# Issuing the first load ahead of the opening barrier in a row-wise maximum-norm kernel

## The chip, the cores and the metric

The kernel runs on one core of one Trainium2 chip. TensorE, VectorE, ScalarE, GpSimd and SyncE are the five engines that have a row of instructions in its trace. The profile counts 16 DMA engines, which carry out the loads and stores in packets (3072 of 64 KB for the bulk loads); here SyncE issues all loads and the last store, ScalarE the two other stores. A barrier is a place in the program where every engine waits until all have reported; a drain is the instruction with which an engine comes to it (SyncE's starts at 0.00 us in the kernel before, and SyncE is released at 0.65). The metric is the device time of an execution in microseconds (us). The profile gives a second number, the span: from the first to the last instruction on record in one profiled execution. Device time and span differ by the same amount in the two profiled runs: 629.88 against 628.10 us before the change, 629.10 against 627.32 after it, which is 1.78 us both times.

## The reference

```python
def setup_inputs():
    return {"x": np.random.randn(8192, 8192).astype(np.float32)}   # rows, cols

def reference(x):
    return np.linalg.norm(x, ord=np.inf, axis=1)
```

`np.linalg.norm` with `ord=np.inf` and one axis is the largest absolute value of each row. The input is 268 MB and the output 32 KB, so the kernel is a stream of loads with one reduction behind it.

## The kernel before

A tile `t` holds two rows for each of 128 partitions (16384 float32 values a partition, 8.39 MB in all). SyncE issues the load, VectorE reduces it; there are three buffers. The first 48 rows of each partition (24 tiles) are the bulk; the last 16 rows are the tail, loaded and reduced in ever smaller pieces so that little work is left when the last data arrive.

```python
TAIL = (
    [[8192]] * 8
    + [[4096, 4096]] * 5
    + [[2048] * 4] * 2
    + [[2048, 2048, 2048, 1024, 512, 512]]
)
# ... (views of x and out; pools: sbuf has bufs=3)
    nc.vector.memset(part[:], 0.0)

    def absmax(o, i):
        nc.vector.reduce_max(out=o, in_=i, axis=X, apply_absolute_value=True)

    for a in range(A):
        for n in range(G):
            t = sbuf.tile([P, B * cols + 16], F32, tag="t")
            nc.sync.dma_start(out=t[:, : B * cols], in_=x_b[a, n])
            absmax(
                r_bulk[:, a, n * B : (n + 1) * B],
                t[:, : B * cols].rearrange("p (b c) -> p b c", b=B),
            )
    nc.scalar.dma_start(out=out_b, in_=r_bulk[:])
    # ... (the tail, in the pieces of TAIL, results into part and then r_tail, r_fin)
```

No line of the kernel function writes the opening barrier. The trace shows it ahead of the program, under the line that makes the program object (L114): GpSimd sets four constants (0.23 to 0.43 us), each engine runs a drain, the four others report with theirs (SyncE's starts at 0.00, TensorE's as the last of them at 0.32), and GpSimd collects the reports at 0.53 and releases the four at 0.61; SyncE goes on at 0.65.

## Time and profile before

| | before |
|---|---|
| device time, median of the first 3 runs | 629.97 us (629.90 to 630.30) |
| span of the profiled run | 628.10 us |
| SyncE released from the opening barrier | 0.65 us |
| first load issued / first packet | 0.73 / 1.75 us |
| bulk reduction starts, one to the next | 19.33 us on average |
| last data in | 623.22 us |
| from last data to the end of the span | 4.88 us |

The barrier's release, the packets and the last data are read from the single records of the trace; everything else is on the page and in the views below. First, lines of the profile page of the kernel before: the span, VectorE's busy time, the busy share of the DMA engines in 40 equal slices (9 is 90% or more), and the bytes moved.

```profile
span 628.1 us, 196 instructions
...
DVE 552.7 (88%) x58; POOL 0.2 (0%) x4
...
DMA  9999999999999999999999999999999999999996
...
HBM read 268.44 MB, written 0.03 MB: 427 GB/s over the span
```

The DMA engines are busy for 90% of the time or more in all slices but the last, where the program ends. From the packet records, the rate between 20 and 460 us is 433.9 GB/s. VectorE is the second busiest, at 88%.

The timeline of the kernel before, first 24 us. Columns are start, duration, engine with line and operation, then what ended the idle time before it. SPq is SyncE's queue of issues; one line may sum up several issues.

```profile
start us, us, engine line op out<-in xcount [idle before <-releaser]
...
0.73 1.33 SPq L68 DMA_DIRECT2D t<-in_x_dram  x3
0.81 0.11 DVE L60 MEMSET part<- 128x60 f32 x1 [0.81 <-PEq L114]
22.83 17.22 DVE L63 TENSOR_REDUCE r_bulk<-t 128x2 f32<-128x16384 f32 x1 [21.91 <-DMA t<-in_x_dram]
```

The first load is issued at 0.73 us, and VectorE then has nothing to do for 21.91 us. The wait view of the kernel before (waiter, line, what it waited for: total us, times, longest):

```profile
DVE r_bulk L63 <- DMA t<-in_x_dram: 70.5, 24, 21.9
```

Of the 70.5 us, the first wait is 21.9; the other 23 are some 2.1 us each. VectorE is ahead of the stream in every bulk tile. The chain of waits of the kernel before, its first pieces (start, duration, what):

```profile
0.66 0.07 issue
0.73 0.38 SPq L68
1.11 0.06 issue
1.17 40.92 DMA t<-in_x_dram
...
42.11 17.22 DVE r_bulk L63
```

Read this view with care. It enters the stream through the *second* load, issued at 1.17 and landed at 42.09, because that is the load for which VectorE waits at 42 us. For the first 20.8 of these 40.92 us the load stands in the queue behind the first one: by the packet records its own first packets start at 21.95 on average. The timeline's end, kernel before:

```profile
621.01 4.01 DVE L63 TENSOR_REDUCE t<-t 128x1 f32<-128x2048 f32 x3 [0.20 <-DMA t<-in_x_dram]
625.05 0.69 DVE L63 TENSOR_REDUCE r_fin<-t 128x1 f32<-128x517 f32 x1
625.77 0.35 SPq L99 DMA_DIRECT2D out_dram<-r_fin  x1
```

### The profile page before, as it was taken

The page shows a single profiled execution, that of the slowest core. Times are in us where ns is not written, and L with a number is a line of the kernel's source. Part 1 is how long each engine was busy: PE and PEld are TensorE (multiplying, and loading weights), DVE is VectorE, ACT ScalarE, POOL GpSimd, SP SyncE. Part 2 cuts the span into 40 slices and gives each one's busy share as a digit, 9 for nine tenths or more (in the row PEclk, how much of TensorE's full clock was granted, in tenths as well). Part 3 has the DMA queues.
Part 4 walks back from the last instruction along what each step waited for, and adds up shares of the span by engine and source line. Part 5 has one row for each costly group of instructions (what it writes and reads, how often), then busy time and mean ns, then how long its engine had stood idle before and what let it go on. Part 6 is the DMA issues. An engine that isn't in the chain of part 4 may idle for free.

```text
span 628.1 us, 196 instructions
## 1 busy us (share of the span) xinstructions
DVE 552.7 (88%) x58; POOL 0.2 (0%) x4
## 2 busy tenths in 40 slices
DVE  0588988889988889888898888998889999999998
POOL 0000000000000000000000000000000000000000
DMA  9999999999999999999999999999999999999996
GB/s 401 413 455 413 455 413 455 413 455 413 455 413 455 409 459 413 455 413 455 413 455 413 455 413 455 413 455 413 455 405 430 434 435 432 420 432 432 424 426 274
DMA packets 9138, 268.49 MB, mean 427 GB/s; under 512 B 1968, under 2 KB 1968, under 8 KB 2352
## 3 DMA queue, kind: packets, MB, share of 16 engines
q1 hardware_dynamic: 8208, 268.44, 99.1%
q10 hardware_dynamic: 928, 0.03, 0.1%
q14 instruction: 2, 0.02, 0.0%
HBM read 268.44 MB, written 0.03 MB: 427 GB/s over the span
## 4 chain that ended last, share of the span: by engine, by line
DMA 64%; DVE 30%; another core or an unknown queue 4%; issue 1%; SPq 0%
DMA t<-in_x_dram 64%; DVE r_bulk L63 23%; DVE part L63 5%; DVE t L63 1%; SPq L82 0%; DVE r_fin L63 0%; SPq L68 0%
## 5 line engine op out<-in xcount | busy, mean ns | idle before, releaser
L63 DVE TENSOR_REDUCE r_bulk<-t 128x2 f32<-128x16384 f32 x24 | 413.3, 17219 | 70.5 <-DMA t<-in_x_dram 70.5
L63 DVE TENSOR_REDUCE part<-t 128x1 f32<-128x4096 f32 (+2 forms) x26 | 130.0, 5067 | 1.3 <-DMA t<-in_x_dram 1.3
L63 DVE TENSOR_REDUCE t<-t 128x1 f32<-128x2048 f32 (+2 forms) x5 | 8.6, 1746 | 0.4 <-DMA t<-in_x_dram 0.4
L60 DVE MEMSET part<- 128x60 f32 x1 | 0.1, 108 | 0.8 <-PEq L114 0.8
L63 DVE TENSOR_REDUCE r_fin<-t 128x1 f32<-128x517 f32 x1 | 0.7, 692 | 0.0
L63 DVE TENSOR_REDUCE r_tail<-part 128x15 f32<-128x60 f32 x1 | 0.2, 216 | 0.0
L114 POOL MEMSET const-bfloat16-1.0<- 128x1 bf16 x1 | 0.1, 101 | 0.0
L114 POOL MEMSET const-uint8-127<- 128x1 uint8 x1 | 0.1, 101 | 0.0
L114 POOL MEMSET const-float32-0.0<- 128x1 f32 x1 | 0.1, 98 | 0.2 <-issue 0.2
L114 POOL MEMSET const-float32-1.0<- 128x1 f32 x1 | 0.1, 98 | 0.0
## 6 DMA issues: line engine op xcount, KB each, us to landing
t<-in_x_dram SPq DMA_DIRECT2D x8, 4096.0 KB, 37.0
t<-in_x_dram SPq DMA_DIRECT2D x10, 2048.0 KB, 30.4
t<-in_x_dram SPq DMA_DIRECT2D x11, 1024.0 KB, 24.6
t<-in_x_dram SPq DMA_DIRECT2D x1, 512.0 KB, 15.9
t<-in_x_dram SPq DMA_DIRECT2D x2, 256.0 KB, 13.2
t<-in_x_dram SPq DMA_DIRECT2D x24, 40.7
out_dram<-r_bulk ACTq DMA_DIRECT2D x1, 24.0 KB, 57.9
out_dram<-r_tail ACTq DMA_DIRECT2D x1, 7.5 KB, 5.6
```

Of the source, the lines that this page charges most:

```text
L60: nc.vector.memset(part[:], 0.0)
L63: nc.vector.reduce_max(out=o, in_=i, axis=X, apply_absolute_value=True)
L114: nc = _bacc.Bacc("TRN2", target_bir_lowering=False, num_devices=1)
```

## The change

The intent: no work of the first load depends on the barrier, so let SyncE issue it as its first instruction. After the program is built, a hook takes the first DMA instruction of SyncE out of its block, asserts that it waits for nothing, and puts it ahead of SyncE's first instruction.

```diff
+def start_first_load_early(nc):
+    sp = mybir.EngineType.SP
+    first, *rest = nc.main_func.blocks
+    for block in rest:
+        insts = block.instructions
+        for i, ins in enumerate(insts):
+            if ins.engine == sp and type(ins).__name__ == "InstDMACopy":
+                assert not ins.sync_info.on_wait
+                moved = insts[i]
+                block.instructions = insts[:i] + insts[i + 1 :]
+                head = first.instructions
+                at = next(k for k, h in enumerate(head) if h.engine == sp)
+                first.instructions = head[:at] + [moved] + head[at:]
+                return
 ...
     nc.sync.dma_start(out=out_t[:, n_tail - 1 :], in_=r_fin[:])
+    nc.at_finalize(start_first_load_early)
```

## The prediction

> **What bounds the kernel now.** The stream of loads. The page shows 268.44 MB in a 628.1 us span (427 GB/s), DMA at 9 tenths or more in all slices but the last. From the packet records, between 20 and 460 us the rate is 433.9 GB/s, one 8.39 MB tile per 19.3 us. [...] VectorE is busy 88%: a bulk reduction takes 17.22 us and then waits 2.1 us for its load (chain and wait views). Three loads are in flight, so when a buffer is released about one and a tenth tiles are still queued: from the first packet at 1.75 us to the last data at 623.2 us there is no moment at which all 16 DMA engines are idle.
>
> So the time is a sum: start to first packet (1.75 us), the stream (621.5 us), the fixed end after it (4.9 us: last reductions, output store, closing barrier), plus 1.8 us by which the device time of the profiled run (629.88) exceeds its span.
>
> **What the change does.** Only the first term changes. Before, SyncE starts at 0.00 with its drain, is released from the opening barrier at 0.65 and issues the first load at 0.73 (0.38 us in the sequencer, first packet 0.64 us after that). Now the load is SyncE's first instruction, at 0.00. The load waits for nothing. Added: SyncE reaches the barrier about 0.38 us later (its drain follows the load), near 0.45 us; GpSimd collects at 0.53 us only after its own memsets, so the barrier moves by 0 to 0.15 us. That delays only the second load, which has 20 us of slack behind the first, and VectorE's memset of the partial maxima, which is needed at 490 us. The second and third loads issue at about 0.75 and 1.2 us instead of 1.17 and 1.64.
>
> **Share on the critical path.** All of the 0.73 us: the stream never runs dry. That is 0.12% of 630 us. [...]
>
> **Predicted time:** 629.97 - 0.73 = 629.25 us; 8 in 10 between 628.95 and 629.8. Faster by over 2%: 0.3%; within 2%: 99.2%; slower by over 2%: 0.5%.
>
> **What the profile would show.** (1) First load at 0.00 in the timeline, first packet near 1.0 instead of 1.75, first reduction at 22.1 instead of 22.83, its first wait shorter by 0.7. (2) The same 19.3 us period, the last data 0.7 us earlier, the same 4.9 us end. (3) Span about 627.4 us. (4) SyncE released from the barrier at 0.65 to 0.8, the second load right after it.
>
> **What would make it wrong.** (a) SyncE's drain might wait for the load's completion, not just its issue: then barrier, second load and all else would be held some 20 us, the stream would have a hole of about 2 us, and the kernel would lose one to two us. (b) The first load may cost more to issue or to start when it is the very first instruction, eating some of the 0.73. (c) The profile's zero is SyncE's first instruction; the device time may begin elsewhere. (d) The gain is only about twice the spread of the three runs (0.4 us).

## The result and the profile after

| | before | after | difference |
|---|---|---|---|
| median device time, 6 runs each | 630.14 us (629.90 to 630.55) | 629.13 us (628.99 to 629.77) | |
| ratio | | 0.9986, 95% interval 0.9973 to 0.9999 | |
| span of the profiled run | 628.10 | 627.32 | -0.78 |
| first load issued | 0.73 | 0.00 | -0.73 |
| SyncE released from the barrier | 0.65 | 0.71 | +0.06 |
| second load issued | 1.17 | 0.79 | -0.38 |
| first packet | 1.75 | 1.02 | -0.74 |
| first reduction starts | 22.83 | 22.03 | -0.80 |
| 24th reduction starts | 467.49 | 466.71 | -0.78 |
| last data in | 623.22 | 622.45 | -0.77 |
| last data to end of span | 4.88 | 4.87 | -0.01 |

A ratio is the mean time of one kernel's runs over the mean of the other's of the same rounds, so it is not quite the ratio of the medians quoted. Here the means are 629.30 and 630.17, 0.87 us apart.

The page after the change, the lines that answer to those above:

```profile
span 627.3 us, 196 instructions
...
DVE 552.7 (88%) x58; POOL 0.2 (0%) x4
...
DMA  9999999999999999999999999999999999999996
...
HBM read 268.44 MB, written 0.03 MB: 428 GB/s over the span
```

The timeline after the change, first 24 us:

```profile
start us, us, engine line op out<-in xcount [idle before <-releaser]
0.00 1.87 SPq L86 DMA_DIRECT2D t<-in_x_dram  x3
...
0.87 0.11 DVE L78 MEMSET part<- 128x60 f32 x1 [0.87 <-PEq L133]
22.03 17.22 DVE L81 TENSOR_REDUCE r_bulk<-t 128x2 f32<-128x16384 f32 x1 [21.05 <-DMA t<-in_x_dram]
```

The first issue is at 0.00, and the line still sums up three issues (0.00, 0.79 and 1.17). VectorE's first own work, the memset, comes 0.06 us later, because the barrier is released later. Its first reduction comes 0.80 us earlier. The wait view after the change:

```profile
DVE r_bulk L81 <- DMA t<-in_x_dram: 69.7, 24, 21.1
```

The total falls by 0.8 us, all of it in the longest wait (21.9 to 21.1). The chain after the change, its first pieces:

```profile
0.72 0.07 issue
0.79 40.50 DMA t<-in_x_dram
...
41.32 17.22 DVE r_bulk L81
```

The chain enters through the second load again, now issued at 0.79. The end of the timeline after the change:

```profile
620.23 4.00 DVE L81 TENSOR_REDUCE t<-t 128x1 f32<-128x2048 f32 x3 [0.19 <-DMA t<-in_x_dram]
624.26 0.69 DVE L81 TENSOR_REDUCE r_fin<-t 128x1 f32<-128x517 f32 x1
624.98 0.35 SPq L117 DMA_DIRECT2D out_dram<-r_fin  x1
```

Line by line this is the end of before, 0.77 to 0.79 us earlier. So the trace puts the whole difference ahead of the first reduction, and nothing gives it back.

### The profile page after: what moved, and what is told of

The parts are those of the page before. It is cut to its first block, busy times and chain, and to the rows that moved or that the text cites. A ratio compares the mean times of both kernels' runs of the same rounds, so it can differ in the third digit from the quotient of the medians.

```text
span 627.3 us, 196 instructions
## 1 busy us (share of the span) xinstructions
DVE 552.7 (88%) x58; POOL 0.2 (0%) x4
## 4 chain that ended last, share of the span: by engine, by line
DMA 64%; DVE 30%; another core or an unknown queue 4%; issue 1%; SPq 0%
DMA t<-in_x_dram 64%; DVE r_bulk L81 24%; DVE part L81 5%; DVE t L81 1%; SPq L100 0%; DVE r_fin L81 0%
```

## The experiments

The theory: the gain is the advance of the first load's issue, and the stream, which never runs dry, hands it to the end one for one. The rivals:

1. Something else in the edit helps: the load's place in the first block (a block is a stretch of the program's instruction list), or its being the very first instruction.
2. The second and third loads matter, which also move ahead by 0.4 to 0.5 us, and which the chain view names.
3. The difference is chance. It is about as large as the scatter of single runs.

All runs gave the correct result. Times are medians or means of 4 or 5 runs, beside 7 or 9 runs of the kernel before.

### e1: in the first block, behind the barrier

```diff
-at = next(k for k, h in enumerate(head) if h.engine == sp)
+at = next(k for k, h in enumerate(head)
+          if h.engine == sp and type(h).__name__ == "InstUnconditionalBranch")
```

> The first load is moved into the first block as in the change, but behind SyncE's wait on the opening barrier. Theory (the gain is the advance of the first issue, handed on one for one by an unbroken stream): the load issues at about 0.67 instead of 0.73 us, so the span is 628.0 us (628.1 less 0.06) and the time that of the kernel before within 0.15 us. Rival (what helps is that the load stands in the first block, ahead of the branch): a first packet well before 1.69 us and a span near 627.3 us.

Measured: mean 630.04 us against 629.98 for the kernel before, ratio 1.0001 (0.9986 to 1.0016). The load issued at 0.73, not at 0.67 as I had expected: passing the branch saved no time that the records show. The profiled span was 628.37, which misses the expected 628.0; the kernel before has such spans too (its timed runs in these rounds had 628.0 to 628.4). The trace puts the excess in the first tile: the first packet starts at 1.72, no later than before, but the first reduction at 23.07 in place of 22.83, and the later ones stay as far behind. What follows: the place in the program is worth nothing as long as the barrier is still ahead. The first half of rival 1 is out.

### e2: ahead of the barrier, behind SyncE's drain

```diff
-at = next(k for k, h in enumerate(head) if h.engine == sp)
+at = 1 + next(k for k, h in enumerate(head)
+              if h.engine == sp and type(h).__name__ == "InstDrain")
```

> The load stands behind SyncE's first drain but still ahead of its wait on the barrier, so SyncE reports to the barrier before it issues. Theory: issue at 0.02 to 0.08 us, first packet at about 1.05, span 627.3 to 627.4 us as in the changed kernel; the barrier is released at about 0.65 again, as before the change, and that is worth nothing. Rival (part of the gain comes from being the very first instruction, or the later barrier costs something): span differs from 627.3 by more than 0.2 us.

The timeline of e2:

```profile
0.08 1.45 SPq L87 DMA_DIRECT2D t<-in_x_dram  x3
```

Measured: issue at 0.08, barrier released at 0.65 as before the change, mean 629.31 us, against 629.30 for the changed kernel in its own rounds. The profiled span, 627.58, is 0.26 above that of the changed kernel, a little more than the 0.2 that I had set; the timed runs had 627.4 to 627.6. The trace puts this excess far from the start: up to the 23rd reduction e2 is at most 0.05 us behind the changed kernel, and from the 24th on 0.24 (466.95 against 466.71). What follows: being the very first instruction is worth no more than the 0.08 us of its issue, and the 0.06 us by which the changed kernel releases its barrier later cost nothing that shows.

### e3: a larger dose the other way

The kernel before, with the first load held back by a memset of its own buffer (the small memsets are meant to keep the scheduler from swapping the loads; the loads kept their order).

```diff
+if a == 0 and n < 3:
+    nc.vector.memset(t[:, : 4096 if n == 0 else 16], 0.0)
 nc.sync.dma_start(out=t[:, : B * cols], in_=x_b[a, n])
```

> The kernel before, with the first load made to wait for a VectorE memset of a part of its buffer, some 2 to 5 us long. Theory: the span grows by exactly the delay of the first issue (issue time less 0.73), within 0.15 us; with an issue at 5.2 us the span is 632.6 us. Rival (a start-up of a few us is hidden somewhere in 620 us of stream, and the 0.78 us gained was chance): the span grows by less than half of the delay.

The timeline of e3:

```profile
5.22 1.32 SPq L70 DMA_DIRECT2D t<-in_x_dram  x3
27.25 17.22 DVE L63 TENSOR_REDUCE r_bulk<-t 128x2 f32<-128x16384 f32 x1 [22.01 <-DMA t<-in_x_dram]
```

Measured: the issue moved by 4.49 us (0.73 to 5.22), the span by 4.69 (628.10 to 632.79), the mean time by 4.70 (629.98 to 634.68). The first reduction and the 24th both start 4.42 us later than before. So the delay goes through the 24 bulk tiles without loss. The last 0.27 us is added in the tail, after the 24th reduction; my margin of 0.15 us was missed by 0.05, and I have no explanation for that part. What follows: the dose is six times that of the change, far outside the scatter, and the answer is one for one. Rival 3 is out as to the mechanism. The second and third loads moved with the first here (to 5.64 and 6.12 us); e4 tells them apart.

### e4: the second load late, but in time

The changed kernel, with the second load (and with it the third) held back by a GpSimd memset.

```diff
+if a == 0 and n == 1:
+    nc.gpsimd.memset(t[:, :8192], 0.0)
 nc.sync.dma_start(out=t[:, : B * cols], in_=x_b[a, n])
```

> The changed kernel, with the second load (and with it the third) held back by a GpSimd memset of half of its buffer, to an issue near 9 us or later instead of 0.79. Theory: the first tile keeps the DMA engines busy until 21 us, so as long as the second issue falls before about 20 us the span stays 627.3 us within 0.2. Rival (the gain comes from the second and third loads, which the change also moves ahead by 0.4 to 0.5 us): the span is longer, by at least the 0.8 us that the change gained.

The timeline of e4 (the SPq line runs from the first issue to the end of the third):

```profile
0.00 8.53 SPq L88 DMA_DIRECT2D t<-in_x_dram  x3
...
0.77 6.92 POOL L87 MEMSET t<- 128x8192 f32 x1 [0.33 <-POOLq L135]
...
22.15 17.22 DVE L81 TENSOR_REDUCE r_bulk<-t 128x2 f32<-128x16384 f32 x1 [21.19 <-DMA t<-in_x_dram]
```

Measured: the second load issued at 7.72 us in place of 0.79, and the time was 629.50 us on average (629.18 to 629.82). That is 0.20 above the changed kernel's mean in the first comparison and 0.34 above its mean in e8, neither of the same rounds. Rival 2 asked for at least 0.8 us. The packet records show that no hole opens: the second tile's first packets start at 21.14 us on average over the 16 engines, against 21.15 in the unmodified changed kernel run beside later experiments. The profiled span was 627.66, 0.34 above the changed kernel and outside my 0.2. The first reduction is already 0.12 us later than in the changed kernel, the second 0.34, and the 24th 0.26. The records place the second tile's share at a single lagging engine (the third tile's first packets start at 40.50 on average in e4 and 40.51 in the unmodified kernel, but the latest one at 41.28 against 41.03), not at a hole. Whether the late issue has a part in this, or it is scatter like that of the first tile in e1, stays open. What follows: 6.9 us of delay to the second load cost 0.2 to 0.35 us, so 0.38 us of advance to it cannot be the gain of 0.8. The chain view names a load whose issue time hardly matters here.

### e5: three loads ahead of the barrier

```diff
-            if ins.engine == sp and type(ins).__name__ == "InstDMACopy":
+            if (len(moved) < 3 and ins.engine == sp
+                    and type(ins).__name__ == "InstDMACopy"):
 ...
-                first.instructions = head[:at] + [moved] + head[at:]
+    first.instructions = head[:at] + moved + head[at:]
```

> The first three loads, not one, are moved to SyncE's first instructions; the barrier is then held up until SyncE has issued all three, to about 1.5 us. Theory: the first issue is at 0.00 as in the changed kernel and nothing else counts, so the time is that of the changed kernel, 629.3 us on average, within 0.2, span 627.3 us within 0.3. Rival (the advance of the later loads gives a part of the gain): 0.3 us or more below the changed kernel. Second rival (a later barrier costs): longer by the 0.8 us that the barrier moves.

Measured: the second and third loads issued at 0.42 and 0.88, the barrier was released at 1.64 (0.93 us later than in the changed kernel), and the mean was 629.25 us (629.12 to 629.52) against 629.16 for the changed kernel in the same rounds (e8). The profiled span was 627.74, outside my 0.3. The trace does not put this at the start: the first five reductions start 0.06 to 0.09 us earlier than in e8, and 0.47 us is lost between the fifth and the ninth. What follows: rival 2 falls a second time, and the barrier's release, too, can move by almost a microsecond at no cost that shows.

### e6: the second load too late

```diff
+if a == 0 and n in (1, 2):
+    for _ in range(2):
+        nc.gpsimd.memset(t[:, :12288], 0.0)
 nc.sync.dma_start(out=t[:, : B * cols], in_=x_b[a, n])
```

> The changed kernel with the second load held back by GpSimd memsets until about 32 us, past the end of the first tile (whose pieces land at 21.5 us on average in the changed kernel). Theory: the DMA engines have nothing to do from about 21.5 us to the first packet of the second tile, about 33 us, and the whole hole of 11.5 us is added: span 638.8 us, within 0.5. Rival (some start-up time is absorbed later, since VectorE is only 88% busy and three buffers are there): less than half of the hole is seen.

The timeline of e6 (GpSimd's line sums up four memsets; the second load could go after the third of them):

```profile
0.00 42.76 SPq L89 DMA_DIRECT2D t<-in_x_dram  x4
...
0.77 41.16 POOL L88 MEMSET t<- 128x12288 f32 x4 [0.33 <-POOLq L136]
...
21.96 17.22 DVE L81 TENSOR_REDUCE r_bulk<-t 128x2 f32<-128x16384 f32 x1 [21.00 <-DMA t<-in_x_dram]
53.66 17.22 DVE L81 TENSOR_REDUCE r_bulk<-t 128x2 f32<-128x16384 f32 x1 [14.48 <-DMA t<-in_x_dram]
```

Measured: second issue at 31.68 us, span 640.14, mean 641.75 against 629.16 for the changed kernel run beside it (e8): 12.6 us more on the clock, 12.8 in the profiles. I had expected 11.5 within 0.5. The sum was short in two terms. The engines were idle for 11.88 us on average (first tile's last packets end at 21.14, the second's first ones start at 33.02, each a mean over 16 engines). And the stream starts slowly again: the first packet of each engine takes 2.79 us on average in place of the 2.42 of later ones (2.87 at the start of the changed kernel, where these packets also begin 0.3 us after the earliest on average, at 1.36 against 1.02 us), and the second tile takes 0.37 us longer from first start to last end (19.73 against 19.36). That is 12.25; the remaining 0.56 of the profiled difference is added bit by bit later in the stream and in the tail, and I cannot assign it. What follows: a hole in this stream is paid in full and with a surcharge. VectorE's 12% of free time and the three buffers absorb none of it.

### e7 and e8: an attempt at a faster kernel, beside the changed one

e8 is the changed kernel, unmodified. e7 changes the pieces of the last row:

```diff
-    + [[2048, 2048, 2048, 1024, 512, 512]]
+    + [[2048, 1536, 1280, 1024, 896, 768, 640]]
```

> An attempt at a faster kernel: the changed kernel with the last row cut into pieces of 2048, 1536, 1280, 1024, 896, 768, 640 columns in place of 2048, 2048, 2048, 1024, 512, 512. In the changed kernel the last data arrive at 622.45 us but VectorE starts its last reduction only at 624.26, being a 1024 and a 512 piece behind. With pieces that shrink slowly VectorE should be at most a few tenths behind: last reduction about 1.0 us after the last data instead of 1.8, and the same stream. Expected span 626.3 us (626.0 to 626.9), about 0.8 to 1.2 us below the changed kernel. If small pieces slow the stream instead, the last data arrive later than 622.6 us and the gain is smaller.

> The changed kernel again, on this chip, beside the kernel before and the others. Theory: mean about 0.8 us below the kernel before (629.2 to 629.4 against 630.0 to 630.2), span of the profiled run 627.2 to 628.0. If the gain had been chance, the two would agree within 0.3 us.

e8 came out as expected: mean 629.16 us against 629.99 for the kernel before, 0.83 us less, span 627.33. Its interval (ratio 0.9988, 0.9974 to 1.0001) just reaches one; the scatter is that of the kernel before, whose nine runs lie between 629.72 and 630.58.

e7 was a miss: mean 629.09 (628.79 to 629.62), span 627.01, so 0.07 and 0.32 us below e8 where 0.8 to 1.2 was expected. The two ends, e8 first:

```profile
593.23 21.96 DVE L81 TENSOR_REDUCE part<-t 128x1 f32<-128x4096 f32 x9 [0.48 <-DMA t<-in_x_dram]
...
615.36 4.69 DVE L81 TENSOR_REDUCE t<-t 128x1 f32<-128x2048 f32 x2
...
620.24 4.00 DVE L81 TENSOR_REDUCE t<-t 128x1 f32<-128x2048 f32 x3 [0.18 <-DMA t<-in_x_dram]
624.27 0.69 DVE L81 TENSOR_REDUCE r_fin<-t 128x1 f32<-128x517 f32 x1
```

```profile
593.27 21.96 DVE L81 TENSOR_REDUCE part<-t 128x1 f32<-128x4096 f32 x9 [0.35 <-DMA t<-in_x_dram]
...
615.40 8.31 DVE L81 TENSOR_REDUCE t<-t 128x1 f32<-128x2048 f32 x6
...
623.74 0.82 DVE L81 TENSOR_REDUCE r_fin<-t 128x1 f32<-128x646 f32 x1
```

The first line's wait (0.48 and 0.35 us) stands ahead of its first reduction. After that VectorE waits twice in e8, for 0.13 and 0.18 us by the single records, and not at all in e7. VectorE is busy for 31.35 of the 32 us from 593 to 625 us in e8. So over the last 30 us VectorE has as little room as the stream, and other pieces can win back only these waits, three tenths in all. My expectation looked at the last two pieces only and took VectorE for idle ahead of them. To gain more there, its work over the whole tail has to shrink, or be shared. I did not find a kernel clearly faster than the changed one.

### e9 to e12: where the early load should be worth nothing

If the theory is right, the same edit must gain nothing when the first thing that everything waits for is not the stream. e9 is the kernel before and e10 the changed kernel, both with VectorE kept busy at its start (the store of r_bulk is adapted to it, not shown):

```diff
-r_bulk = outp.tile([P, A, G * B], F32)
+wide = outp.tile([P, 3072], F32)
+for _ in range(24):
+    nc.vector.memset(wide[:], 0.0)
+r_bulk = wide[:, : A * G * B].rearrange("p (a m) -> p a m", a=A)
```

> The kernel before with VectorE made busy for about 60 us at its start (24 memsets of a scratch tile that the first reduction must follow). The three buffers fill by about 60 us and the stream then stands still until VectorE's first reduction, so the start of everything after hangs on VectorE, which starts at the release of the opening barrier (0.81 us) and not on the first load. Expected span about 628 plus 20 to 30 us; the exact number only matters beside the next run.

> The changed kernel with the same 60 us of VectorE work at its start. Theory (the gain is worth the advance of the first load only where the stream is what everything waits for): no gain over e9_busy_before; the barrier is released 0.04 to 0.06 us later, so the span is equal or up to 0.1 us longer, and the medians agree within 0.3 us. Rival (the early start gains 0.7 us by itself, wherever the critical path runs): 0.7 to 0.8 us below e9_busy_before.

The memsets took longer than estimated (to 80 us, with 0.7 us between them), which changes nothing in the comparison. The timeline of e9, then of e10:

```profile
0.73 114.54 SPq L71 DMA_DIRECT2D t<-in_x_dram  x5
...
77.92 2.62 DVE L57 MEMSET wide<- 128x3072 f32 x1 [0.71 <-DVE wide L57]
80.57 51.47 DVE L66 TENSOR_REDUCE wide<-t 128x2 f32<-128x16384 f32 x3
```

```profile
0.00 115.31 SPq L89 DMA_DIRECT2D t<-in_x_dram  x5
...
77.96 2.62 DVE L75 MEMSET wide<- 128x3072 f32 x1 [0.71 <-DVE wide L75]
80.61 51.47 DVE L84 TENSOR_REDUCE wide<-t 128x2 f32<-128x16384 f32 x3
```

The first load goes out at 0.73 and at 0.00, and VectorE's first reduction starts at 80.57 and at 80.61: with the early load it is 0.04 us *later*, as is its first memset behind the barrier (1.48 against 1.44). The spans are 667.34 and 667.35. The packet records show where the advance went: the three buffers are full and the DMA engines are all idle from 61.15 us on in e9 and from 60.36 in e10, and both start again at 98.78 and 98.81. The 0.8 us has become a longer wait.

The timed runs are less clear: medians 669.47 and 669.15, 0.32 apart, between what the theory (0.3 at most) and the rival (0.7 to 0.8) asked for.

> The pair of e9 and e10 again, in the other order and with more rounds, because their medians differed by 0.32 us where the profiles' spans agreed to 0.02 us. This is the one with the early load. Theory: its mean is within 0.2 us of that of the next run. Rival: 0.7 to 0.8 us below it.

> The one without the early load, with VectorE busy at its start. Theory: within 0.2 us of the run before, span about 667.3 us. Rival: 0.7 to 0.8 us above it.

Means 669.20 with the early load and 669.60 without; profiled spans 667.65 and 667.41, the other way round. The lowest runs of all four are 669.05 and 669.13 with, 669.11 and 669.19 without. Pooled, the means are 669.22 (9 runs) and 669.58 (8 runs), 0.36 apart, which is half of what the rival asks. The floors agree within 0.06 us, while the kernels without the early load more often had runs some 0.3 to 1.1 us above it. By means, my margin of 0.2 is missed. The four traces show no gain from the start, since all streams restart within 0.07 us of each other, those with the early load last (98.81 and 98.83 against 98.78 and 98.76); why the upsets were more frequent in these 8 runs than in the 9 others, or whether that is chance, stays open.

One trace shows where such an upset can arise. The profiled run of e11 is its slowest (669.43 us). Its first nine reductions start 0.02 us behind those of e10; then it falls behind in steps, to 0.12 us at the 10th, to 0.18 at the 20th and to 0.3 in the tail, and makes hardly any of it up. The excess of e2 and e5 came in the same way. So a loss in mid-stream, too, is carried to the end. The slow runs of e9 and e12 were not profiled, so where they lost their time is not shown.

## Why the prediction was right

The prediction of 629.25 us (range 628.95 to 629.8) met a median of 629.13. The number alone proves little: 6 of the 38 runs of the kernel before lie inside the range, too. What bears the account are the terms. Point by point:

- **Sum of start, stream and end.** Right. In the trace the start to the first packet shrank by 0.74, the stream from first packet to last data took 621.47 us before and 621.44 after, the end 4.88 and 4.87.
- **All of the advance is on the critical path.** Right, and shown: e3 returned 4.42 us at the last bulk tile for a 4.49 us delay of the issue, and in the traces of e9 to e12 the gain is gone when VectorE's start takes the stream's place. By the clock this second half is not settled: 0.36 us is left between the means.
- **Size, 0.73 us.** The profiles differ by 0.78: 0.73 from the issue, and the rest arises in the first tile, which was complete 20.99 us after the first packet, against 21.05 before. The medians of the first comparison differ by 1.01 us and the means by 0.87, both above 0.73. Pooled over all rounds, the kernel before has a median of 629.93 (38 runs, lowest 629.72) and the changed one of 629.17 (11 runs, e8 among them, lowest 628.99): 0.76 and 0.73 apart. The prediction's size stands, and the excess of the first comparison is scatter.
- **Barrier later by 0 to 0.15 us, near 0.45 us for SyncE's report.** The release moved by 0.06 us. SyncE's drain began at 0.43, but took 0.13 us behind the load in place of 0.01, so it reported at about 0.56, and GpSimd, ready at 0.53 before the change, collected at 0.59. The time of the report was off by 0.1, inside the stated slack.
- **Second load has 20 us of slack.** Right: e4 used 6.9 us of it and lost 0.2 to 0.35 us, not the 0.8 of the gain, and e6, past the end of the slack, paid more than the hole.
- **The four dangers.** (a) SyncE's drain does not wait for the load to land: it ended at 0.56 us, the load landed at 22.0. (b) The issue as first instruction took the same 0.38 us, and the first packet came 1.02 us after the start of the issue in both kernels (0.64 and 0.63 us after its end). (c) The device time less the span is 1.78 us in both, so the device time saw the whole advance. (d) Was real: the 95% interval of the first comparison ends at 0.9999.

## What to carry to other kernels

In this kernel, one unbroken stream, what lay ahead of the first load was paid in full (e3: 4.49 us of delay, 4.42 at the last bulk tile), so in one like it a load that waits for nothing belongs ahead of the program's opening barrier; but only the first one, since the second queued behind it with a whole tile of slack here (19.3 us; 6.9 us of delay to it cost 0.2 to 0.35 us in e4). Ask first whether the stream is what the rest waits for: with another engine's work in front, the same edit moved the first load by 0.73 us, but in four traces not the restart of the stream (the timed means, 0.36 us apart, leave a part of this open). And a gain of 0.1% is near the scatter of single runs: believe it from the trace, reduction by reduction, and from a larger dose of the same cause, not from one median.
